# Sums of squares, the spread of the norm factors and the order of low parts in a two-layer hybrid encoder

## The chip, the cores and the metric

The kernel runs on one core of one Trainium2 chip. The metric is the device time of one execution in microseconds (us). The kernel before has a median of 2450.57 us over three runs (2447.43 to 2455.9). The engines are called PE (matmul), DVE (vector), ACT (scalar), POOL (general) and SP (issues DMAs); a DMA is called by the queue that issues it.

## The reference

The input is 256 and 512 tokens of width 1024 (one sequence each, 768 tokens together), all in fp32. There are two layers and a final norm:

```
x = x + concat_sum( sigmoid(gate_n) * branch_n( mixer_n( rmsnorm(x) ) ), n = A, B, C ) @ w_out
g, v = split( conv3( rmsnorm(x) @ w_up ) )        # each D_FF = 2816 wide
x = x + ( silu(g) * v ) @ w_down
y = rmsnorm(x) * final_g
rmsnorm(x) = x * rsqrt(mean(x*x) + 1e-6) * g
```

Mixer A is a chunked spatial gate, mixer B a windowed grouped-query attention with a sink and a relative bias, mixer C a grouped-query attention with normed and rotated queries and keys. What matters here is the norm: five times (two in each layer, one at the end, that one in two parts) the squares of x are summed over 1024 channels, a factor r is made for each token, and r is spread over all 128 partitions so that it can be multiplied onto rows of channels.

## The kernel before

Activations lie transposed: x is eight tiles of 128 channels by 768 tokens. Every fp32 product is done as three passes of a reduced format (fp32r): a value is split in a high part (`wh`, `u[:, 0]`), written by ACT as a copy, and a low part (`wl`, `u[:, 1]`), written by DVE as the difference, and PE adds high·high, high·low and low·high. For the weights a class `Stream` does this along a fixed plan: `split` (L296) issues ACT's copy (L337 or L327), `flush` (L354) issues DVE's difference (L357) and then the DMA of the next weight on SP. `dense` (L426) is the loop of matmuls L435 over k steps; it calls `flush` after one of its first k steps, and after each step lets background generators (attention, the closing norm) and delayed work (the convolution of the FFN) issue a piece. So the order in which DVE meets low parts, attention steps and convolution steps is the order in which this Python code calls them, and no scheduler changes it.

Norms. ACT squares a tile (`sumsq`, L499 and L502) and the tiles are added: in the first norm partly by DVE, partly by POOL (L504); in the others by DMAs on POOL's queue that accumulate (L508) into two sums, closed by DVE (L504, L506). `rstd_tok` (L510) sums over channels by small matmuls with ones (L514), DVE scales (L517) and POOL takes the power (L520). `rstd_bc` (L523) spreads r: for each 128 tokens DVE makes a diagonal `dg` (L534, two buffers), PE multiplies it with ones (L535, fp32), ACT copies it out (L537).

Layer phases: the token-major projections `dense_tok` (matmuls L554, evacuated by ACT L586), the attentions as background of gate and branch products, then `layer_out` (L963): evacuation L1005, and for each of four pairs of tiles operands `ua`, `ub`, `un`, `ut` (sums and differences of halves, each with a high part by ACT, L985/L987, and a low part by DVE, L988) for the FFN's up products. These are seven half-size products P1 to P7 in place of eight (matmuls L1109, evacuated by ACT L1117 and others). Up products run in 22 groups; down products (`dn`) follow in eight chunks, evacuated by DVE (L1168, in the last layer's last chunk L1158, then multiplied by the final factor in L1234). At the change of layers `prep` (L487) makes high and low parts of the new x (L488, L489) and its squares (L502).

Buffers: `page` gives one of 7 tiles of 128 x 768, `unit` one of 23 tiles twice that size, which also hold x and the operands.

Of the kernel before, what the change touches and what calls it, by code (L numbers as in the profile page):

```python
# [10 lines left out]
F32 = mybir.dt.float32  # L11
# [7 lines left out]
P = 128  # L19
# [110 lines left out]
def encoder_kernel(ctx, tc, x_d, w_d, vec_d, ln_d, rope_d, gqk_d, oneh_d, relb_d, mask_d, id_d, y_d):  # L130
# [65 lines left out]
    identr = const.tile([P, P], F32R, name="identr")  # L196
    ones = const.tile([P, P], F32, name="ones")
    neghalf = const.tile([P, 24], F32, name="neghalf")
# [4 lines left out]
    class Stream:  # L203
# [92 lines left out]
        def split(self, parts=1):  # L296
# [3 lines left out]
            if e[0] in ("pc", "down"):  # L300
# [11 lines left out]
                if e[:3] == ("down", DEPTH - 1, len(FFC) - 1):  # L312
                    k = None
                    if e[3] % 2 == 0:
                        st["keep"] = unit()
                    h, l2 = (st["keep"][:, e[3] % 2, i * HT:i * HT + w] for i in range(2))
                elif self.open is None:
                    k = j
                    hi, lo = self.pair()
                    self.open = (k, hi, lo)  # L320
                    h, l2 = hi[:, 0:w], lo[:, 0:w]
                else:
                    k, hi, lo = self.open
                    self.open = None
                    h, l2 = hi[:, 512:512 + w], lo[:, 512:512 + w]
# [100 lines left out]
    def dense(ps, hi, lo, off, ks, xs, first, last, cuts=(0, 384, 768), mid=None):  # L426
        nk = len(ks)
        for i, (kw, kx) in enumerate(ks):
# [11 lines left out]
            if mid is not None and i == 3:  # L440
                mid()
            if i == min(2, nk - 1):
                W.flush()
# [9 lines left out]
    def load_consts():  # L453
        DVE.memset(ones, 1.0)
        DVE.memset(zero, 0.0)
        DVE.memset(neghalf, -0.5)
        POOL.dma_start(out=ident, in_=id_d)
# [29 lines left out]
    def prep(x_ap, g, xu, k):  # L487
        ACT.activation(xu[:, 0], x_ap, AF.Identity, scale=g)  # L488
        DVE.scalar_tensor_tensor(xu[:, 1], x_ap, g, fl(xu[:, 0]), ALU.mult, ALU.subtract)  # L489
        if k is not None:  # L490
            sumsq(x_ap, k)

    def sumsq(x_ap, k, dve=None):

        n = x_ap.shape[-1]
        c = k % 2 if dve is None else 0
        if k == c:
            st["acc", c] = page()[:, 0:n]
            ACT.activation(st["acc", c], x_ap, AF.Square)  # L499
            return  # L500
        sq = page()[:, 0:n]
        ACT.activation(sq, x_ap, AF.Square)  # L502
        if dve is not None or k >= KD - 2:
            (POOL if dve is False else DVE).tensor_tensor(st["acc", 0], st["acc", 0], sq, ALU.add)  # L504
            if dve is None and k == KD - 2:
                DVE.tensor_tensor(st["acc", 0], st["acc", 0], st.pop(("acc", 1)), ALU.add)  # L506
# [3 lines left out]
    def rstd_tok(n=NT):  # L510
# [10 lines left out]
        st["rt"] = r  # L521

    def rstd_bc(n=NT, gap=False):  # L523
        r = st["rt"]
        bc = page(776) if gap else page()
        if gap:
            POOL.memset(bc[:, 513:514], 0.0)
        for a, b in ((0, min(n, 4)), (4, n)):
            if a >= b:
                continue  # L530
            ps = sps()
            for t in range(a, b):
                dg = sm.tile([P, P], F32, tag="dg", name=nm("dg"), bufs=2)
                DVE.tensor_scalar(dg, ident, r[:, t:t + 1], None, ALU.mult)  # L534
                PE.matmul(out=ps[:, (t - a) * P:(t - a + 1) * P], lhsT=ones, rhs=dg, start=True, stop=True)  # L535
            o = 1 + (a > 0) if gap else 0
            ACT.activation(bc[:, o + a * P:o + b * P], ps[:, 0:(b - a) * P], AF.Copy)  # L537
        st["bcg" if gap else "bc"] = bc
# [29 lines left out]
    def layer_mixers(l, xs):  # L568
# [15 lines left out]
        for c in range(2):  # L584
# [4 lines left out]
            if c == 0:  # L589
                ACT.activation(small(2)[:, 0:1], neghalf[:, 0:1], AF.Gelu_apprx_tanh)  # L590
            dense_tok(("in2", l, 512 + c * 256, 0), ("in2", l, 512 + c * 256, 1), xs, evac_v,
                      rstd_tok if c == 0 else None, kouter=c == 0)
        rt = st["rt"]
# [369 lines left out]
    def layer_out(l, mhl, x_src, x_mid):  # L963
# [29 lines left out]
        for i in range(4):  # L993
# [4 lines left out]
            for q in range(2):  # L998
# [12 lines left out]
                else:  # L1011
                    hl2(h3(xa), ub, g, slice(0, 2))
                    DVE.scalar_tensor_tensor(ta[:, HT:T], xa[:, HT:T], g, xg[:, HT:T], ALU.mult, ALU.subtract)
                    DVE.tensor_tensor(tb[:, 0:HT], ta[:, HT:T], xg[:, 0:HT], ALU.add)
                    DVE.scalar_tensor_tensor(tb[:, HT:T], xa[:, 0:HT], g, tb[:, 0:HT], ALU.mult, ALU.subtract)
                    hl2(h3(tb), un, -1.0, slice(0, 2))
                    hl2(ta[:, HT:T], ut, 1.0, i % 2)
                sumsq(xa, m)
                POOL.dma_start(out=x_mid[m], in_=xa)
# [6 lines left out]
    def layer_ffn(l, xs2, x_mid, x_spill):  # L1026
# [125 lines left out]
        def evac(c, m, cuts, ps):  # L1152
            last = c == len(FFC) - 1
            final_ = last and l == DEPTH - 1
            if final_:
                t0, t1 = cuts
                xa = st["xu"][m // 2][:, m % 2, t0:t1]
                DVE.tensor_tensor(xa, ps[:, 0, 0:t1 - t0], xa, ALU.add)  # L1158
                sumsq(xa, m)
                if t0 and m == 2:  # L1160
# [18 lines left out]
        for s in steps:  # L1179
            if s[0] == "pc":  # L1180
                piece(s[1], s[2])
                if (s[1], s[2]) == (0, "P5"):
                    rstd_tok()
                elif (s[1], s[2]) == (1, "P1"):
                    rstd_bc(gap=True)
# [33 lines left out]
    def final(xu, t0, t1):  # L1219
        n = (t1 - t0) // P  # L1220
        ph["ffn"] = "end"
        if t0 == 0:
            yield
            yield
        rstd_tok(n)
        if t0 == 0:
            yield
        yield
# [10 lines left out]
    with tc.manual_schedule():  # L1239
# [17 lines left out]
        for k in range(KD):  # L1257
# [15 lines left out]
            if k > 2:  # L1273
                sumsq(xu[(k - 3) // 2][:, (k - 3) % 2], k - 3, k % 2 == 0)
        for k in range(KD - 3, KD):
            sumsq(xu[k // 2][:, k % 2], k, True)
        del u, xu
# [137 lines left out]
```

## Time and profile before

| | us |
|---|---|
| median of three runs | 2450.57 |
| the profiled execution | 2452.3 |
| its span | 2450.1 |
| PE busy | 2393.8 |
| DVE busy | 1531.0 |
| ACT busy | 1106.6 |
| POOL busy | 268.2 |

The profile is of one execution, with a mean granted clock of 0.988. PE is busy for 98% of the span, so the time is PE's work, its idle stretches, and those stretches in which it runs on the lower of its two clocks (a granted clock of 0.5 is 1.2 GHz, of 1.0 is 2.4 GHz). A duration of a few matmuls in a row in the timeline is their span together.

### The profile page before, as it was taken

To read this page: it belongs to the slowest core of one execution; us is meant where nothing else is said; L and a number is where in the kernel's file an instruction comes from. 1 tells how busy PE (TensorE), PEld (TensorE's weight loads), DVE (VectorE), ACT (ScalarE), POOL (GpSimd) and SP (SyncE) were. 2 spreads that over 40 slices of the span, in tenths; PEclk is the share of its full clock that TensorE was granted. 3 is DMA by queue.
4 is the path that set the end of the run, shared out by engine and by line. 5 is a ranking of instruction groups with operands and counts; after the bars stand their busy time and mean duration, and the time that the engine had idled before them with its cause. 6 is when DMAs were issued, how large, how long until landed. Compare 5 with 4: busy or idle time off the path is not lost.

```text
span 2450.1 us, 38743 instructions
## 1 busy us (share of the span) xinstructions
PE 2393.8 (98%) x15030; PEld 2325.3 (95%) x15030; DVE 1531.0 (62%) x2691; ACT 1106.6 (45%) x2186; POOL 268.2 (11%) x396
## 2 busy tenths in 40 slices
PE   9999999999999999999999999999999999999996
PEld 8999999899999999999899999998999999999996
DVE  5555446554568777777645554555446688777774
ACT  4344444652355444444433543466424544444441
POOL 2000110000121111111000001100001211111101
PEclk9999999999999999999999999999999999999997
DMA  4411221112568998887722113111135699888865
GB/s 145 105 59 51 51 74 44 35 43 88 163 145 237 257 239 228 230 222 207 234 90 61 58 51 63 61 44 36 44 119 155 150 273 241 241 229 233 223 170 169
DMA packets 142439, 340.82 MB, mean 139 GB/s; under 512 B 16809, under 2 KB 34857, under 8 KB 142257
## 3 DMA queue, kind: packets, MB, share of 16 engines
q1 hardware_dynamic: 108144, 264.41, 33.0%
q0 software_dynamic: 34112, 73.95, 17.1%
q8 instruction: 118, 1.93, 0.3%
q14 instruction: 65, 0.52, 0.1%
HBM read 250.22 MB, written 58.72 MB: 126 GB/s over the span
## 4 chain that ended last, share of the span: by engine, by line
PE 85%; DMA 5%; DVE 3%; ACT 3%; issue 3%; POOL 0%; SPq 0%; POOLq 0%; DVEq 0%; ACTq 0%
PE d L435 46%; PE ga L1109 13%; PE gb L1109 9%; PE d L554 7%; PE s L799 3%; PE s L786 3%; PE s L747 3%; DMA raw<-w_pk 1%; DMA pg<-gqk 1%; PE s L659 1%; DMA qd<-qc 1%; DVE wl L357 1%; DMA qc<-w_pk 0%; DMA u<-w_pk 0%; ACT wh L327 0%
## 5 line engine op out<-in xcount | busy, mean ns | idle before, releaser
L435 PE MATMUL d<-u,wh 128*128 128x384 f32 x4512 | 996.6, 342 | 5.4 <-ACT pg L1074 5.0
L435 PEld LDWEIGHTS d<-u,wh 128*128 128x128 f32 x4512 | 788.1, 188 | 20.3 <-issue 11.0
L435 PE MATMUL d<-u,wl 128*128 128x384 f32 x2256 | 579.5, 338 | 0.0
L435 PEld LDWEIGHTS d<-u,wl 128*128 128x128 f32 x2256 | 410.7, 188 | 0.0
L1109 PE MATMUL ga<-u,wh 128*128 128x384 f32 x1408 | 364.6, 340 | 12.3 <-ACT u L1117 7.2
L357 DVE TENSOR_TENSOR wl<-raw,wh 128x512 fp32r<-128x512 f32 (+1 forms) x261 | 248.1, 951 | 200.9 <-ACT wh L337 155.4
L1109 PE MATMUL gb<-u,wh 128*128 128x384 f32 x1056 | 271.9, 339 | 0.9 <-DVE u L1119 0.9
L1109 PEld LDWEIGHTS ga<-u,wh 128*128 128x128 f32 x1408 | 257.1, 189 | 14.3 <-ACT u L1117 7.9
L554 PE MATMUL d<-wh,u 128*128 128x256 f32 x1344 | 249.1, 285 | 7.5 <-DVE pg L1168 3.2
L1109 PE MATMUL ga<-u,wl 128*128 128x384 f32 x704 | 238.9, 339 | 0.0
L554 PEld LDWEIGHTS d<-wh,u 128*128 128x128 f32 x1344 | 211.4, 191 | 9.7 <-issue 3.5
L1109 PEld LDWEIGHTS gb<-u,wh 128*128 128x128 f32 x1056 | 192.6, 189 | 1.2 <-ACT u L1083 1.2
L554 PE MATMUL d<-wl,u 128*128 128x256 f32 x672 | 190.8, 284 | 2.0 <-DVE wl L357 2.0
L337 ACT ACTIVATE wh<-raw 128x1024 fp32r<-128x1024 f32 x129 | 135.3, 1050 | 103.3 <-PE d L554 47.6
L1109 PE MATMUL gb<-u,wl 128*128 128x384 f32 x528 | 178.3, 338 | 0.0
L1168 DVE TENSOR_TENSOR pg<-d,pg 128x768 f32<-128x768 f32 x120 | 114.6, 955 | 90.8 <-PE d L435 85.6
L1046 ACT ACTIVATE pg<-u,vec 128x769 f32<-128x769 f32 x88 | 90.9, 1033 | 99.3 <-DVE u L1054 65.8
L1109 PEld LDWEIGHTS ga<-u,wl 128*128 128x128 f32 x704 | 133.3, 189 | 0.0
L554 PEld LDWEIGHTS d<-wl,u 128*128 128x128 f32 x672 | 128.6, 191 | 2.6 <-DVE wl L357 2.4
L652 DVE TENSOR_TENSOR u<-s,u 128x128 fp32r<-128x128 f32 (+1 forms) x112 | 36.8, 329 | 120.6 <-ACT u L651 120.4
L747 PE MATMUL s<-u,u 128*128 128x256 f32 (+2 forms) x384 | 99.9, 342 | 0.0
L1109 PEld LDWEIGHTS gb<-u,wl 128*128 128x128 f32 x528 | 99.7, 189 | 0.0
(197 smaller groups left out, 3142.1 us busy)
## 6 DMA issues: line engine op xcount, KB each, us to landing
raw<-w_pk SPq DMA_DIRECT2D x174, 512.0 KB, 3.7
pg<-xm SPq DMA_DIRECT2D x120, 384.0 KB, 5.1
xm<-pg SPq DMA_DIRECT2D x112, 384.0 KB, 3.9
u<-w_pk SPq DMA_DIRECT2D x96, 192.0 KB, 3.5
qa<-w_pk SPq DMA_DIRECT2D x44, 256.0 KB, 4.5
qb<-w_pk SPq DMA_DIRECT2D x44, 256.0 KB, 3.2
qc<-w_pk SPq DMA_DIRECT2D x44, 256.0 KB, 3.7
qd<-w_pk SPq DMA_DIRECT2D x44, 256.0 KB, 3.6
```

What stands on the lines that cost most here:

```text
L337: ACT.activation(hi[:, :n], t[:, :n], AF.Copy)
L357: DVE.tensor_tensor(lo, t, fl(hi), ALU.subtract)
L435: PE.matmul(out=ps[:, h, 0:b - a], lhsT=w, rhs=x[:, a:b], start=first and i == 0 and pi == 0, stop=last and i == nk - 1 and pi == 2,)
L554: PE.matmul(out=outs[t], lhsT=x, rhs=w, start=k == 0 and pi == 0 and t % 2 == 0, stop=k == KD - 1 and pi == 2, skip_group_check=True)
L652: DVE.tensor_tensor(u[:, 1, a:b], ps, fl(u[:, 0, a:b]), ALU.subtract)
L659: PE.transpose(o.bitcast(F32R) if idn is identr else o, srcs(t), idn)
L747: PE.matmul(out=ps[:, 0:w], lhsT=q, rhs=kb[:, c, lo * P:hi * P], start=c == 0, stop=c == 1)
L786: PE.transpose(ps[:, b * P:(b + 1) * P], lg[:, b * P:(b + 1) * P], ident)
L799: PE.matmul(out=ps[e * HD:(e + 1) * HD, 0:P], lhsT=vtok[:, (lo + b) * P + kv * HD:(lo + b) * P + (kv + 1) * HD], rhs=pT, start=b == 0, sto ...
L1046: ACT.activation(f, h[:, 1:770], AF.Identity, scale=cw(1, ct), bias=vec[:, VCB + ct:VCB + ct + 1])
L1109: PE.matmul(out=o, lhsT=a[:, w], rhs=x[:, b], start=p in ("P1", "P2", "P5") and kp == 0 and pi == 0, stop=kp == 3 and pi == 2, skip_group_ ...
L1168: DVE.tensor_tensor(h2(xa), ps[:, :, 0:384], h2(xa), ALU.add)
```

## The change

The eight chunks of the down product stay. Seven things change:

1. `dense` calls `flush` after the first k step where it has at most four (branch products and down chunks), not after the third or last.
2. In the first norm the squares of tiles 2 to 5 are accumulated by four DMAs on POOL's queue into two sums; DVE adds the last two and the second sum. POOL's and DVE's earlier additions go.
3. In the last layer's closing norm DVE adds all squares, and no DMA does.
4. The factors are spread by one 768-wide product on DVE, split in two fp32r parts, and four matmuls (two of 512 and two of 256 columns) with fp32r ones (`onesr`), in place of six diagonals and six fp32 matmuls. In the closing norm the matmuls stand one step of the background (three matmuls) later.
5. At the change of layers the squares lie in a `unit`, not a `page`.
6. In `layer_out` the operands of the second tile of a pair are made in another order, `un` in two halves.
7. In the last layer's last down chunk each weight has a `unit` of its own.

```diff
@@ Stream.split
                 if e[:3] == ("down", DEPTH - 1, len(FFC) - 1):
                     k = None
-                    if e[3] % 2 == 0:
-                        st["keep"] = unit()
-                    h, l2 = (st["keep"][:, e[3] % 2, i * HT:i * HT + w] for i in range(2))
+                    u = unit()
+                    h, l2 = u[:, 0, 0:w], u[:, 1, 0:w]
@@ dense
-            if i == min(2, nk - 1):
+            if i == (2 if nk > 4 else 0):
                 W.flush()
@@ load_consts
+        DVE.tensor_scalar(onesr, ones[:, 0:1].broadcast_to([P, P]), 1.0, None, ALU.mult)
@@ prep, sumsq
         if k is not None:
-            sumsq(x_ap, k)
+            sumsq(x_ap, k, new=lambda: unit(F32)[:, 0])
 
-    def sumsq(x_ap, k, dve=None):
+    def sumsq(x_ap, k, dve=False, new=None):
 
         n = x_ap.shape[-1]
-        c = k % 2 if dve is None else 0
+        c = 0 if dve else k % 2
+        sq = (new or page)()[:, 0:n]
+        ACT.activation(sq, x_ap, AF.Square)
         if k == c:
-            st["acc", c] = page()[:, 0:n]
-            ACT.activation(st["acc", c], x_ap, AF.Square)
+            st["acc", c] = sq
             return
-        sq = page()[:, 0:n]
-        ACT.activation(sq, x_ap, AF.Square)
-        if dve is not None or k >= KD - 2:
-            (POOL if dve is False else DVE).tensor_tensor(st["acc", 0], st["acc", 0], sq, ALU.add)
-            if dve is None and k == KD - 2:
+        if dve or k >= KD - 2:
+            DVE.tensor_tensor(st["acc", 0], st["acc", 0], sq, ALU.add)
+            if not dve and k == KD - 2:
                 DVE.tensor_tensor(st["acc", 0], st["acc", 0], st.pop(("acc", 1)), ALU.add)
         else:
             POOL.dma_start(out=st["acc", c], in_=sq, accum_op=ALU.add)
@@ rstd_diag, rstd_bc
+    def rstd_diag(n=NT):
+
+        r = st["rt"]
+        dh, dl = page(T, F32R)[:, 0:n * P], page(T, F32R)[:, 0:n * P]
+        dg = page()[:, 0:n * P]
+        i3 = ident.unsqueeze(1).broadcast_to([P, n, P])
+        r3 = r[:, 0:n].unsqueeze(2).broadcast_to([P, n, P])
+        DVE.tensor_tensor(dg.rearrange("p (t n) -> p t n", n=P), i3, r3, ALU.mult)
+        ACT.activation(dh, dg, AF.Copy)
+        DVE.tensor_tensor(dl, dg, fl(dh), ALU.subtract)
+        st["dg"] = dh, dl
+
     def rstd_bc(n=NT, gap=False):
-        r = st["rt"]
...
-            for t in range(a, b):
-                dg = sm.tile([P, P], F32, tag="dg", name=nm("dg"), bufs=2)
-                DVE.tensor_scalar(dg, ident, r[:, t:t + 1], None, ALU.mult)
-                PE.matmul(out=ps[:, (t - a) * P:(t - a + 1) * P], lhsT=ones, rhs=dg, start=True, stop=True)
+            for i, d in enumerate(st["dg"]):
+                PE.matmul(out=ps[:, 0:b - a], lhsT=onesr, rhs=d[:, a:b], start=i == 0, stop=i == 1)
@@ layer_mixers
-                      rstd_tok if c == 0 else None, kouter=c == 0)
+                      rstd_tok if c == 0 else rstd_diag, kouter=c == 0)
@@ layer_out, half, the branch for q == 1
-                    hl2(h3(xa), ub, g, slice(0, 2))
+                    ACT.activation(ub[:, 0:2, 0], h3(xa), AF.Identity, scale=g)
                     DVE.scalar_tensor_tensor(ta[:, HT:T], xa[:, HT:T], g, xg[:, HT:T], ALU.mult, ALU.subtract)
                     DVE.tensor_tensor(tb[:, 0:HT], ta[:, HT:T], xg[:, 0:HT], ALU.add)
+                    DVE.scalar_tensor_tensor(ub[:, 0:2, 1], h3(xa), g, fl(ub[:, 0:2, 0]), ALU.mult, ALU.subtract)
+                    hl2(tb[:, 0:HT], un, -1.0, 0)
                     DVE.scalar_tensor_tensor(tb[:, HT:T], xa[:, 0:HT], g, tb[:, 0:HT], ALU.mult, ALU.subtract)
-                    hl2(h3(tb), un, -1.0, slice(0, 2))
                     hl2(ta[:, HT:T], ut, 1.0, i % 2)
+                    hl2(tb[:, HT:T], un, -1.0, 1)
@@ layer_ffn, evac
-                sumsq(xa, m)
+                sumsq(xa, m, dve=True)
@@ layer_ffn, steps
                 if (s[1], s[2]) == (0, "P5"):
                     rstd_tok()
+                    rstd_diag()
@@ final
         rstd_tok(n)
+        rstd_diag(n)
         if t0 == 0:
+            yield
             yield
         yield
         rstd_bc(n)
@@ the kernel's start
             if k > 2:
-                sumsq(xu[(k - 3) // 2][:, (k - 3) % 2], k - 3, k % 2 == 0)
+                sumsq(xu[(k - 3) // 2][:, (k - 3) % 2], k - 3)
         for k in range(KD - 3, KD):
-            sumsq(xu[k // 2][:, k % 2], k, True)
+            sumsq(xu[k // 2][:, k % 2], k)
```

How this moves DVE's instructions is shown at three places. First the start, where the first norm's sum closes: `u` at L489 (L490 in the changed kernel) is a low part of x, `pg` at L504 and L506 are additions of squares, L517 reads the finished sum. Before:

```order
L489 SCALAR_TENSOR_TENSOR u_164<-u_99,vec_91,u_164 128x768
L357 TENSOR_TENSOR wl_168<-raw_107,wh_167 128x1024
L489 SCALAR_TENSOR_TENSOR u_176<-u_100,vec_91,u_176 128x768
L504 TENSOR_TENSOR pg_156<-pg_156,pg_179 128x768
L489 SCALAR_TENSOR_TENSOR u_182<-u_100,vec_91,u_182 128x768
L504 TENSOR_TENSOR pg_156<-pg_156,pg_188 128x768
L504 TENSOR_TENSOR pg_156<-pg_156,pg_191 128x768
L504 TENSOR_TENSOR pg_156<-pg_156,pg_194 128x768
```

In the changed kernel:

```order
L490 SCALAR_TENSOR_TENSOR u_165<-u_101,vec_92,u_165 128x768
L357 TENSOR_TENSOR wl_169<-raw_109,wh_168 128x1024
L490 SCALAR_TENSOR_TENSOR u_177<-u_102,vec_92,u_177 128x768
L490 SCALAR_TENSOR_TENSOR u_183<-u_102,vec_92,u_183 128x768
L504 TENSOR_TENSOR pg_158<-pg_158,pg_192 128x768
L506 TENSOR_TENSOR pg_158<-pg_158,pg_163 128x768
L504 TENSOR_TENSOR pg_158<-pg_158,pg_196 128x768
L357 TENSOR_TENSOR wl_228<-raw_156,wh_227 128x1024
```

The additions among the low parts are gone, and of the three that are left the first two take sums that DMAs write.

Second the windowed attention of layer 0 (time 211 to 215 before). L836 evacuates a gate product, L770 and L774 (L780 and L784 after) divide a softmax row, L756 (L766) makes the next one, L357 is the low part of a weight. Before:

```order
L836 TENSOR_TENSOR pg_2143<-d_2006,pg_733 128x768
L770 RECIPROCAL sm_2102<-sm_2102 128x1
L774 TENSOR_SCALAR pg_2100<-pg_2100,sm_2102 128x256
L756 ISA pg_2168,sm_2169<-s_2171,sd_1485,sm_576 128x256
L756 ISA sm_2169 128x1
L357 TENSOR_TENSOR wl_2147<-raw_1908,wh_2146 128x1024
```

In the changed kernel:

```order
L846 TENSOR_TENSOR pg_2137<-d_2000,pg_741 128x768
L357 TENSOR_TENSOR wl_2141<-raw_1902,wh_2140 128x1024
L780 RECIPROCAL sm_2096<-sm_2096 128x1
L784 TENSOR_SCALAR pg_2094<-pg_2094,sm_2096 128x256
L766 ISA pg_2165,sm_2166<-s_2168,sd_1479,sm_584 128x256
L766 ISA sm_2166 128x1
```

The low part has moved in front of the division, the next row's start and what follows them.

Third the end: the last rows of the first part of the closing norm. L1158 (L1170 after) adds a down product to x, L504 and L506 add squares, L517 reads the sum. Before:

```order
L1158 TENSOR_TENSOR u_22899<-d_23111,u_22899 128x512
L1158 TENSOR_TENSOR u_22900<-d_23125,u_22900 128x512
L504 TENSOR_TENSOR pg_23038<-pg_23038,pg_23136 128x512
L506 TENSOR_TENSOR pg_23038<-pg_23038,pg_23056 128x512
L1158 TENSOR_TENSOR u_22900<-d_23140,u_22900 128x512
L504 TENSOR_TENSOR pg_23038<-pg_23038,pg_23151 128x512
L517 TENSOR_SCALAR sm_23169<-ga_23164 128x4
```

In the changed kernel:

```order
L1170 TENSOR_TENSOR u_22885<-d_23102,u_22885 128x512
L504 TENSOR_TENSOR pg_23026<-pg_23026,pg_23113 128x512
L1170 TENSOR_TENSOR u_22886<-d_23116,u_22886 128x512
L504 TENSOR_TENSOR pg_23026<-pg_23026,pg_23127 128x512
L1170 TENSOR_TENSOR u_22886<-d_23130,u_22886 128x512
L504 TENSOR_TENSOR pg_23026<-pg_23026,pg_23141 128x512
L517 TENSOR_SCALAR sm_23159<-ga_23154 128x4
```

Each product is now followed by the addition of its square, and no L506 (the second sum, which DMAs filled) stands in front of the last product.

## Rows read from the trace of the kernel before

**Rows 1.** The page, part 1: busy time, share and instructions by engine.

```profile
PE 2393.8 (98%) x15030; PEld 2325.3 (95%) x15030; DVE 1531.0 (62%) x2691; ACT 1106.6 (45%) x2186; POOL 268.2 (11%) x396
```

**Rows 2.** Windows: us, busy (x instructions) by engine, granted clock, DMA share, GB/s.

```profile
20.00:25.00 5.00, 3.84 (x20) 3.84 (x21) 3.07 (x5) 4.69 (x6) 3.54 (x3) 0.66 0.14 38
...
693.00:702.00 9.00, 7.16 (x29) 7.17 (x29) 5.03 (x8) 4.41 (x10) 1.74 (x2) 0.62 0.54 139
...
1213.00:1222.00 9.00, 5.79 (x28) 5.50 (x27) 5.72 (x6) 3.92 (x5) 1.96 (x3) 0.65 0.89 244
...
2412.00:2451.00 39.00, 18.86 (x91) 17.27 (x89) 17.29 (x39) 4.92 (x11) 5.22 (x7) 0.65 0.37 104
```

**Rows 3.** Waits of PE: line, releaser, us in total, times, longest.

```profile
PE ga L514 <- DVE pg L504: 8.8, 2, 5.2
...
PE ga L1109 <- ACT u L1117: 7.2, 2, 3.6
...
PE d L435 <- ACT pg L1074: 5.0, 2, 2.5
...
PE d L554 <- DVE pg L1168: 3.2, 1, 3.2
```

**Rows 4.** Timeline, first norm, ACT, DVE, PE: start, us, instruction, [idle <-releaser].

```profile
16.71 0.83 ACT L502 ACTIVATE pg<-u 128x768 f32<-128x768 f32 x1
...
16.84 2.46 DVE L489 SCALAR_TENSOR_TENSOR u<-u,vec,u 128x768 fp32r<-128x768 f32 x1
...
22.82 3.08 DVE L504 TENSOR_TENSOR pg<-pg,pg 128x768 f32<-128x768 f32 x3 [1.72 <-POOL pg L504]
...
25.96 1.50 PE L514 MATMUL s<-ones,pg 128*128 128x2 f32 x12
...
32.76 0.38 PE L554 MATMUL d<-wh,u 128*128 128x256 f32 x1 [0.93 <-ACT u L586]
```

**Rows 5.** DMA issues: KB, median us to landing; then line L508's range.

```profile
pg<-pg POOLq DMA_DIRECT2D x12, 384.0 KB, 4.5
...
DMA to landing us min/median/max: 2.6/4.3/6.6
```

**Rows 6.** Timeline of PE: spread of factors (layer 0), last chunk's products.

```profile
63.93 0.61 PE L535 MATMUL s<-dg,ones 128*128 128x128 f32 x4
...
66.04 0.36 PE L554 MATMUL d<-wh,u 128*128 128x256 f32 x1
...
2394.45 17.99 PE L435 MATMUL d<-u,u 128*128 128x512 f32 x81
```

**Rows 7.** Timeline of DVE and PE in layer 0's windowed attention.

```profile
211.30 0.15 DVE L770 RECIPROCAL sm<-sm 128x1 f32<-128x1 f32 x1
...
213.40 1.23 DVE L357 TENSOR_TENSOR wl<-raw,wh 128x1024 fp32r<-128x1024 f32 x1 [0.40 <-ACT wh L337]
...
213.24 0.38 PE L786 MATMUL s<-ident,pg 128*128 128x128 f32 x2
```

**Rows 8.** Timeline of DVE, ACT, PE from layer 0's projection into its FFN.

```profile
691.19 0.62 DVE L1015 SCALAR_TENSOR_TENSOR pg<-u,vec,pg 128x384 f32<-128x384 f32 x1
...
691.90 1.25 ACT L985 ACTIVATE u<-pg 128x768 fp32r<-128x768 f32 x2 [2.92 <-DVE pg L1015]
...
694.84 1.01 PE L1109 MATMUL ga<-u,wh 128*128 128x384 f32 x2 [3.60 <-ACT u L1117]
```

**Rows 9.** Timeline of ACT and DVE before PE's 2.48 us wait at 1180.13.

```profile
1172.65 0.51 ACT L327 ACTIVATE wh<-u 128x384 fp32r<-128x384 f32 x1
...
1176.58 0.55 DVE L357 TENSOR_TENSOR wl<-u,wh 128x384 fp32r<-128x384 f32 x1
```

**Rows 10.** Timeline of ACT before layer 1's first matmul.

```profile
1212.51 0.84 ACT L502 ACTIVATE pg<-pg 128x768 f32<-128x768 f32 x1 [1.99 <-DMA sp<-pg]
```

**Rows 11.** Timeline of DVE in the two closing norms.

```profile
2413.29 0.69 DVE L504 TENSOR_TENSOR pg<-pg,pg 128x512 f32<-128x512 f32 x1 [3.30 <-DMA pg<-pg]
...
2437.45 0.42 DVE L506 TENSOR_TENSOR pg<-pg,pg 128x256 f32<-128x256 f32 x1 [1.34 <-DMA pg<-pg]
```

More of the change, by code (lines that the diff above doesn't have):

```diff
@@ L196, in encoder_kernel @@
     identr = const.tile([P, P], F32R, name="identr")
-    ones = const.tile([P, P], F32, name="ones")
+    ones = const.tile([P, 2], F32, name="ones")
+    onesr = const.tile([P, P], F32R, name="onesr")
     neghalf = const.tile([P, 24], F32, name="neghalf")
@@ L527, in rstd_bc @@
             POOL.memset(bc[:, 513:514], 0.0)
-        for a, b in ((0, min(n, 4)), (4, n)):
+        for a, b in ((0, min(n, 4) * P), (4 * P, n * P)):
             if a >= b:
@@ L531, in rstd_bc @@
             ps = sps()
-            for t in range(a, b):
-                dg = sm.tile([P, P], F32, tag="dg", name=nm("dg"), bufs=2)
-                DVE.tensor_scalar(dg, ident, r[:, t:t + 1], None, ALU.mult)
-                PE.matmul(out=ps[:, (t - a) * P:(t - a + 1) * P], lhsT=ones, rhs=dg, start=True, stop=True)
+            for i, d in enumerate(st["dg"]):
+                PE.matmul(out=ps[:, 0:b - a], lhsT=onesr, rhs=d[:, a:b], start=i == 0, stop=i == 1)
             o = 1 + (a > 0) if gap else 0
-            ACT.activation(bc[:, o + a * P:o + b * P], ps[:, 0:(b - a) * P], AF.Copy)
+            ACT.activation(bc[:, o + a:o + b], ps[:, 0:b - a], AF.Copy)
+        del st["dg"]
         st["bcg" if gap else "bc"] = bc
```

## The prediction

> **What bounds the kernel now.** I read the page's busy times first. PE is busy for 2393.8 of 2450.1 us; no other engine is above 62% [rows 1]. So only three things can change the time: what PE executes, where PE waits, and where it runs at the lower clock. The windows by stage show the third: granted 1.00 nearly everywhere, but 0.66 just before the first norm's sum, 0.62 at the entry to an FFN (both layers alike), 0.65 at the change of layers and 0.65 over the last 39 us [rows 2]. Each of these stands at one of PE's longer waits, listed next: 8.8 us in the two closing norms for a sum of squares, 7.2 us at the two FFN entries for ACT, 5.0 us at the end of each layer, 3.2 us at the change of layers [rows 3]. The change works on all four places and, by the order, on attention.
>
> **First norm (start): a loss, +4.8.** Before, DVE closes the sum with three additions from 22.82 on, and PE's L514 starts at 25.96; the first matmul that needs nothing from it but evacuated PSUM follows at 32.76 [rows 4]. Now two chains of two accumulating DMAs each take the additions. The square of tile 3 is ready at 16.71 + 0.83 = 17.54 [rows 4]; POOL starts its DMA some 0.3 later (an estimate). A 384 KB transfer of this kind takes 4.5 us at the median [rows 5], and the next in the chain may start only after it has landed: 17.85 + 4.5 + 0.3 + 4.5 = 27.15. Two of DVE's additions follow it at 3.08 / 3 = about 0.95 apart, so L514 starts near 29.1, 3.1 us late. What goes is POOL's addition, beside which DVE's L489 took 2.46 us [rows 4]; PE then has its inputs sooner, but ends up waiting at L514 anyway, for some 6.5 us. After a wait of 3.6 us PE ran at the lower clock for most of 9 us at 0.62 [rows 2, 3]: 3.4 us of full clock, of which I count 2.7 on work. From L514 to the end of the work that was queued before 32.76 there are 32.76 − 25.96 − 0.93 = 5.8 us of PE, so 29.1 + 5.8 + 2.7 = 37.6, against 32.76: +4.8. At the shortest landing of 2.6 L514 starts at 25.3 and, with half the clock loss, the cost is 0; at the longest of 6.6 it starts at 33.3: +9 [rows 5].
>
> The Trainium skill (SBUF — State Buffer, section "SBUF: two separate sides", the box on DVE blocking DMA) says that a DMA from POOL's queue needs its descriptors written by GpSimd, and that this stalls while DVE holds the shared port. By that rule each link could wait for one of DVE's low parts, about 1 us, and the sum would be 2 us worse. The rows give L508's landing only with DVE at work beside it, so such a stall is in the 4.5 already and I add nothing.
>
> **The spread of the factors, −2.8 −0.8.** In the mixers L535 holds PE from 63.93 to 66.04, 2.1 us, and six DVE products stand between its matmuls [rows 6]. Four fp32r matmuls over 512, 512, 256 and 256 columns cost, at 17.99 / 81 = 0.222 us for 512 [rows 6], 0.22 + 0.22 + 0.11 + 0.11 = 0.67. Their operands (a 768-wide DVE product, an ACT copy, a DVE low part, under 3 us together) can be made from 32.76 on, 31 us before the spread [rows 4, 6], so nothing waits: −1.4 in each layer. In the FFN the power is ready only shortly before the spread, and product, copy and low part then stand in front of PE in one chain; I take −0.4 in each layer, between −1 and +1.5.
>
> **Attention: low parts earlier, +2.1.** In 14 places of the branch products the order moves a low part before a softmax division. It needs ACT's high part first. At 213.40 DVE had waited for that copy already, while the division stood at 211.30: it now goes to 213.4 + 1.2, 3.3 us later, and PE's use of its row at 213.24 is only 1.9 behind the old start [rows 7]. PE is in order, so I estimate 0.8 us lost there after what the matmuls between absorb. At most places the high part is long there, the delay is the 1.2 us of one low part, and PE's next use lies 1 to 3 us behind. I take 0.15 us for each place, 2.1 together; from 0 to the full 14 × 1.23 = 17 us, the trace bounds it no closer.
>
> **Into the FFN, −3.8.** Before, the last operand's two copies start at 691.90, only after L1015 began at 691.19, and ACT's next in line (a square, a weight copy, L1117) let PE go at 694.84 [rows 8]. With L988's full low part (1 us) out of the way of the differences and `un` in halves, only the second half's copy, 1.25 / 2, stands last and starts near 691.45: PE restarts near 693.8, −1.05 in each layer. The wait of 3.6 becomes 2.5. A shorter wait may leave a shorter stretch at the low clock: of the 3.4 us that it takes there [rows 2] I count a quarter back, −0.85 in each layer, between 0 and −2.7.
>
> **End of each layer, +1.5.** PE's wait at 1180.13 (2.5) hangs on an evacuation queued on DVE behind convolution steps. The low part at 1176.58, whose high part was ready at 1172.65 + 0.51 [rows 9], now stands before those steps: about +0.65 in each layer (0.55 and its start), +0.2 together for the clock. In the other FFN groups PE's next use lies several us behind and I count zero; if that cover were gone, some 40 down products at 0.5 each would cost 20 us, which is in no range below.
>
> **Change of layers, −4.0.** At 1212.51 ACT's square had idled 1.99 us until a spill's DMA let a page go [rows 10]; behind it stood the high part of layer 1's first weight, and PE's wait of 3.2 [rows 3]. With squares in units that idle goes: −2.0. The wait that is left is 1.2. Of the 0.35 × 9 = 3.2 us that the low clock takes here [rows 2] most may come back; but before the first norm's sum a low clock stands beside short waits too [rows 2], so I count −2.0. Bounds −1 (the next page is as late) and −5.
>
> **The tail, −3.5.** DVE waited 3.30 us for an accumulating DMA at 2413.29 and 1.34 at 2437.45, with the last product's evacuation queued behind [rows 11]. With additions in place a product's chain is low part, evacuation, ACT's square and addition, each near the 0.69 of an addition [rows 11]: about 2.5 us while low parts stand between and 2.0 after, against PE's 9 × 0.222 = 2.0 [rows 6], so DVE falls behind by some 2 us at most and has nearly caught up at the last product. PE's last matmul ends at 2394.45 + 17.99 = 2412.44 [rows 6]; evacuation, square and addition of 2.0 and a backlog of 0.4 put L514 at 2414.8, a wait of 2.4 for 5.2 [rows 3]. DVE's multiplications by the factor (L1234) still hold the second part's evacuations, so not all of that returns: −1.5 at the middle, −3.5 at the end. Bounds −1.5 (DVE's backlog stays) and −5.5 (the lower clock also ends sooner).
>
> **Sum.** 4.8 − 2.8 − 0.8 + 2.1 − 3.8 + 1.5 − 4.0 − 3.5 = −6.5. Against the profiled execution (2452.3; span 2450.1) this is 2445.8; that execution lies 1.7 above the median of the runs, so the median goes to 2444.
>
> **The rivals.**
> *All clock returns.* At FFN entry and change of layers the waits fall under what costs the clock, and attention hides its low parts: −3.7 more at the entries, −1.2 at the change, −2.1, and the tail's −2: 2444 − 9 = 2435. For it: every one of these waits is shortened. Against it: 2.5 is left at the entries, as long as waits that cost clock before.
> *Gains turn into new waits.* ACT's chain at the entry ends on the square, not the copy; DVE becomes the tail's bound with three operations for each product; the freed page waits on the next spill. Terms at their small ends: 4.8 − 2.8 + 0.5 + 2.1 − 1 + 1.5 − 1 − 1.5 = +2.6, or 2453; since not all three go together, I put it midway between that and my sum: 2448.5. For it: each step has a next one close behind [rows 8, 10]. Against it: they are different engines at different places.
> *Slower: low parts hold the softmax.* One place, 14 times: DVE waits in order for ACT's high part, and PE for the row behind it. At 1.2 us in each place, the length of a low part, this costs 17 in place of 2.1: 2459. The kernel is slower than before from (6.5 + 2.1) / 14 = 0.6 us in each place, and by over 0.3% from (6.5 + 2.1 + 7.35) / 14 = 1.1. For it: DVE idles for ACT's copies at this point already [rows 7]. Against it: most high parts are ready.
> *DMA chain held by DVE* (the rule named above): L514 near 31, +2: 2446. The rows show no such stall by itself.
>
> **How the numbers follow.** A measurement of this kernel can tell 0.3%, 7.35 us, from no change: faster is below 2443.2, slower above 2457.9. My forecast has a chance of 0.46, and its own range of 2437 to 2450 lies about evenly on either side of 2443.2: 0.23 faster, 0.23 same. All clock returns: 0.19, faster. New waits: 0.18, same. DMA chain held: 0.04, same. Low parts hold the softmax: 0.13, slower. Together faster 0.42, same 0.45, slower 0.13. The range starts below the first rival and ends short of the slow one: 2433 to 2454.
>
> **What would show it.** In the changed profile: L514 at the start near 29 (my chain of DMAs right) or before 26 (wrong); L535 of 0.7 us; FFN entries near 2.5 us of wait and a granted clock there above 0.62; the first matmul of layer 1 with a wait near 1.2 at full clock; L514 in the tail with a wait under 3; in attention, waits of PE for L774's and L787's users no more than 2 us above before. I am wrong if PE's waits in attention grow by 10 us, if L514 at the start is later than 33, or if the tail's sum still waits over 4 us.

## The result and the profile after

The changed kernel is slower: 2461.2 us (median of 12 runs) against 2447.66 for the kernel before on the same chip, a ratio of 1.0055, 95% interval [1.0046, 1.0063]. That is +13.5 us where −6.5 was forecast, outside the range. The profiled execution took 2465.5 us, its span is 2463.7.

Part 1 of its page. It answers to [rows 1]: PE does 40 matmuls and 2.8 us less, and the span is 13.6 us longer, so the loss is in PE's idle time: 72.7 us of the span against 56.3.

```profile
PE 2391.0 (97%) x14990; PEld 2319.5 (94%) x14990; DVE 1535.8 (62%) x2688; ACT 1111.2 (45%) x2200; POOL 260.2 (11%) x390
```

Windows of the changed kernel, columns as in [rows 2]: the start, the entry into the FFN of layer 0, the spread of the factors behind it, the change of layers, the tail.

```profile
20.00:45.00 25.00, 13.44 (x82) 13.03 (x81) 8.02 (x13) 8.08 (x13) 5.74 (x8) 0.73 0.60 134
...
714.00:722.00 8.00, 7.17 (x45) 7.17 (x46) 4.00 (x7) 2.89 (x7) 1.73 (x2) 1.00 0.61 166
...
722.00:736.00 14.00, 10.90 (x46) 9.97 (x45) 5.44 (x9) 5.62 (x12) 4.06 (x5) 0.76 0.60 113
...
1230.00:1245.00 15.00, 12.96 (x98) 12.46 (x97) 9.98 (x11) 8.42 (x11) 2.06 (x4) 1.00 0.97 274
...
2426.00:2463.00 37.00, 20.14 (x100) 17.51 (x98) 20.38 (x43) 7.14 (x15) 1.73 (x2) 0.70 0.24 85
```

PE's longest waits, as [rows 3]:

```profile
PE s L514 <- DVE pg L504: 10.6, 1, 10.6
...
PE d L435 <- ACT pg L1086: 6.4, 2, 3.2
...
PE d L564 <- DVE wl L357: 6.2, 2, 3.9
...
PE ga L1121 <- ACT u L1129: 4.4, 2, 2.2
...
PE ga L544 <- ACT pg L531: 3.6, 2, 2.0
...
PE d L544 <- ACT pg L531: 3.6, 2, 2.9
...
PE ga L514 <- DVE pg L504: 3.5, 2, 2.0
...
PE d L564 <- DVE pg L1180: 2.0, 2, 1.2
```

The waits of [rows 3] are all shorter but one: 8.8 us for the closing sums became 3.5, 7.2 at the FFN entries 4.4, 3.2 at the change of layers is in the 2.0; 5.0 at the ends of the layers became 6.4. What is new stands beside them: 10.6 us at the first norm, 6.2 us for a low part, 3.6 us for the FFN's spread (`d L544`) and 3.6 us for the spread in the closing norm (`ga L544`; before, PE waited 1.7 us there for `dg`). And the clock moved with the waits: 0.62 at the entry is 1.00, but behind the spread, where it was full speed, it is 0.76; at the change of layers 0.65 is 1.00.

PE runs the same matmuls in the same order in both kernels, but for the spread. So the n-th matmul of one can be set against the n-th of the other, from PE's timelines, and the lag shows where time goes. It sets one execution against one; each lies some 4.5 us above its kernel's median. "Evacuation" is the copy that empties PE's output buffer (PSUM).

| place (first matmul there) | before | after | lag |
|---|---|---|---|
| first matmul that waits for an evacuation behind the first norm | 32.76 | 43.67 | +10.9 |
| behind the spread, layer 0 | 66.04 | 75.56 | +9.5 |
| gate products, before any moved low part | 88.00 | 98.36 | +10.4 |
| windowed attention | 180.61 | 194.25 | +13.6 |
| behind the tables' DMA | 315.36 | 333.87 | +18.5 |
| second attention | 489.98 | 511.62 | +21.6 |
| behind the FFN entry, layer 0 | 700.12 | 717.75 | +17.6 |
| behind the FFN's spread | 711.96 | 733.94 | +22.0 |
| end of the layer | 1181.44 | 1202.14 | +20.7 |
| layer 1, products | 1223.71 | 1239.48 | +15.8 |
| behind the spread, layer 1 | 1271.16 | 1286.20 | +15.0 |
| second attention | 1693.96 | 1713.00 | +19.0 |
| at the FFN entry, layer 1 | 1899.64 | 1917.46 | +17.8 |
| first closing sum | 2417.63 | 2431.58 | +14.0 |
| end of the span | 2450.1 | 2463.7 | +13.6 |

Four steps up make the result: the start, the attentions, the place behind the tables' DMA (transfers `pg<-gqk` on POOL's queue, which both kernels issue alike for mixer C; more at the end of the experiments) and the FFN's spread in layer 0. Within layer 1's FFN the lag also falls to +13.4 at 2039.87 and rises to +16.8 at 2081.84, behind a wait of 1.82 us for a weight's copy that no other run's list of waits has. The start first: POOL, then DVE and PE (start, us, instruction, idle before and releaser).

```profile
16.23 0.87 POOL L508 DMA_DIRECT2D pg<-pg  x1 [14.20 <-ACT pg L499]
...
17.78 0.85 POOL L508 DMA_DIRECT2D pg<-pg  x1 [0.68 <-ACT pg L499]
...
24.43 0.84 POOL L508 DMA_DIRECT2D pg<-pg  x1 [5.81 <-DMA pg<-pg]
...
26.28 0.84 POOL L508 DMA_DIRECT2D pg<-pg  x1 [1.00 <-DMA pg<-pg]
```

```profile
28.40 0.96 DVE L504 TENSOR_TENSOR pg<-pg,pg 128x768 f32<-128x768 f32 x1 [9.04 <-DMA pg<-pg]
...
31.18 0.96 DVE L506 TENSOR_TENSOR pg<-pg,pg 128x768 f32<-128x768 f32 x1 [1.82 <-DMA pg<-pg]
...
33.26 2.72 PE L514 MATMUL s<-ones,pg 128*128 128x2 f32 x12 [10.63 <-DVE pg L504]
...
43.67 0.39 PE L564 MATMUL d<-wh,u 128*128 128x256 f32 x1 [0.93 <-ACT u L596]
```

The first accumulating DMA was issued at 16.23, and the next of its chain could go only at 24.43; the second, from 17.78, held its follower to 26.28. So each took close to 8 us, not 4.5 [rows 5]; the chain of waits (start, us, what) has the second and the fourth:

```profile
17.78 7.97 DMA pg<-pg
...
26.28 4.81 DMA pg<-pg
```

DVE idled 9.04 us for the chain, L514 started at 33.26 instead of 25.96 [rows 4], after a wait of 10.63, and PE worked off what followed at the lower clock: 10.4 us from L514 to the matmul that waits for an evacuation, 6.8 before. This is the one of the prediction's three signs of being wrong that came: L514 later than 33.

A place in the windowed attention, DVE and PE:

```profile
186.88 1.23 DVE L357 TENSOR_TENSOR wl<-raw,wh 128x1024 fp32r<-128x1024 f32 x1 [1.95 <-ACT wh L337]
...
188.02 0.15 DVE L780 RECIPROCAL sm<-sm 128x1 f32<-128x1 f32 x1
...
189.02 0.44 PE L796 MATMUL s<-ident,pg 128*128 128x128 f32 x2 [1.42 <-DVE sm L766]
...
190.15 0.50 PE L757 MATMUL s<-u,u 128*128 128x256 f32 x2 [0.69 <-ACT pg L797]
```

The low part waited 1.95 us for ACT's high part, and the division behind it came at 188.02; PE waited 1.42 us for its row and 0.69 for the next copy, and the clock fell behind that, as the window of 191 to 195 shows (before, PE was busy without a gap over these matmuls, at 1.00):

```profile
191.00:195.00 4.00, 4.00 (x20) 3.22 (x20) 2.51 (x9) 1.64 (x6) 0.00 (x0) 0.57 0.04 14
```

The attention's waits of PE in the list of waits:

```profile
PE s L796 <- DVE sm L771: 2.4, 3, 1.0
...
PE s L796 <- DVE pg L784: 2.2, 3, 1.0
...
PE s L757 <- ACT pg L797: 1.6, 3, 0.7
...
PE s L796 <- DVE sm L766: 1.4, 1, 1.4
```

With low parts as before only the second of these four lines stands in that list (2.2 us, below); the other three are 5.4 us that the new order made, short of the 10 that the prediction named as a sign; smaller waits and the lower clock at the first place make up the rest of what attention lost.

The spread in the FFN of layer 0: POOL, DVE, ACT, PE.

```profile
723.62 0.84 POOL L275 DMA_DIRECT2D qd<-qc  x1 [3.27 <-DMA qc<-w_pk]
...
724.18 1.66 POOL L520 TENSOR_TENSOR sm<-sm,neghalf 128x6 f32<-128x6 f32 x1
...
725.88 0.96 DVE L530 TENSOR_TENSOR pg<-ident,sm 128x768 f32<-128x768 f32 x1 [5.11 <-POOL sm L520]
...
726.87 0.84 ACT L531 ACTIVATE pg<-pg 128x768 fp32r<-128x768 f32 x1 [8.55 <-DVE pg L530]
...
727.76 0.80 PE L544 MATMUL d<-pg,onesr 128*128 128x512 f32 x1 [2.90 <-ACT pg L531]
```

POOL waits for a weight transfer before it takes the power at 724.18. This was so before, at 704.23: POOL is only 1.7 us nearer, by the lag (+19.95 for +21.6), while PE comes 4.0 us nearer. Product, copy and low part follow the power one after the other, and PE, which now comes at full clock from the entry, waits 2.90 us and then loses clock.

The change of layers and the tail gain what was forecast. PE's first matmul of layer 1 waits 1.17 us at full clock:

```profile
1235.06 0.36 PE L564 MATMUL d<-wh,u 128*128 128x256 f32 x1 [1.17 <-DVE pg L1180]
```

In the tail DVE's additions wait only for ACT's squares, and PE's waits for the sums are 2.0 and 1.6 where they were 5.2 and 3.6. Of these 5.3 us PE gives back 1.9 in the waits for the spread (3.6 for 1.7) and 1.5 in one wait for an evacuation (L1170; 3.2 for 1.7).

```profile
2430.84 0.69 DVE L504 TENSOR_TENSOR pg<-pg,pg 128x512 f32<-128x512 f32 x1 [0.74 <-ACT pg L499]
...
2444.89 0.42 DVE L1170 TENSOR_TENSOR u<-d,u 128x256 f32<-128x256 f32 x1
...
2431.58 1.05 PE L514 MATMUL ga<-ones,pg 128*128 128x2 f32 x8 [1.96 <-DVE pg L504]
...
2452.93 0.58 PE L514 MATMUL ga<-ones,pg 128*128 128x2 f32 x4 [1.58 <-DVE pg L504]
```

### The profile page after: what moved, and what is told of

The parts are those of the page before. It is cut to its first block, busy times and chain, and to the rows that moved or that the text cites. A ratio compares the mean times of both kernels' runs of the same rounds, so it can differ in the third digit from the quotient of the medians.

```text
span 2463.7 us, 38666 instructions
## 1 busy us (share of the span) xinstructions
PE 2391.0 (97%) x14990; PEld 2319.5 (94%) x14990; DVE 1535.8 (62%) x2688; ACT 1111.2 (45%) x2200; POOL 260.2 (11%) x390
## 4 chain that ended last, share of the span: by engine, by line
PE 85%; DMA 5%; DVE 4%; ACT 3%; issue 3%; POOL 0%; POOLq 0%; SPq 0%; DVEq 0%; ACTq 0%
PE d L435 46%; PE ga L1121 13%; PE gb L1121 10%; PE d L564 7%; PE s L809 3%; PE s L796 2%; PE s L757 2%; DMA raw<-w_pk 1%; DVE wl L357 1%; DMA qc<-w_pk 1%; DMA pg<-gqk 1%; PE s L669 1%; DMA pg<-pg 1%; ACT wh L337 0%; DMA qd<-qc 0%
## 5 line engine op out<-in xcount | busy, mean ns | idle before, releaser
L357 DVE TENSOR_TENSOR wl<-raw,wh 128x512 fp32r<-128x512 f32 (+1 forms) x261 | 248.2, 952 | 224.0 <-ACT wh L337 180.9
L768 ACT ACTIVATE pg<-pg,sm 128x257 f32<-128x257 f32 (+1 forms) x96 | 52.5, 547 | 109.2 <-DVE sm L766 105.0
```

The costliest lines, as they stand in the source:

```text
L357: DVE.tensor_tensor(lo, t, fl(hi), ALU.subtract)
L768: ACT.activation(lg, lg, AF.Exp, bias=mn, scale=-1.0, accum_out=su)
```

## The experiments

All ratios are to the kernel before on the same chip, with 95% intervals; the changed kernel stands at 1.0055, and one thousandth is 2.45 us.

### What each of two edits costs

Sums of the first norm as before:

```diff
-        if dve or k >= KD - 2:
+        if old is not None:
+            (POOL if old is False else DVE).tensor_tensor(st["acc", 0], st["acc", 0], sq, ALU.add)
+        elif dve or k >= KD - 2:
```

> The changed kernel with the first norm's sums made as before (POOL and DVE additions, no accumulating DMA). Theory: the start alone lost 10.6 us (PE stood 10.6 us later after the first norm than before), because two accumulating DMAs at once share the same DMA engines and each needs about 8 us; so this run is about 10.5 us below the changed kernel: 2450.5, L514 near 26. Rival: the changed kernel's profiled execution had a late DMA by chance and the start costs the forecast 4.8: 2456.4.

Measured: 1.0025 [1.0013, 1.0037], 7.4 us below the changed kernel, between the two. L514 starts at 25.81 and the matmul behind the next evacuation at 32.61, so the start gives back all of its 10.9; some 3 us are lost again from 88 on, where PE now waits for an evacuation and the clock falls.

Low parts as before:

```diff
-            if i == (2 if nk > 4 else 0):
+            if i == min(2, nk - 1):
```

> The changed kernel with low parts issued after the third or last k step as before. Theory: low parts in front of the softmax cost 6.4 us in layer 0 and 4.0 in layer 1, and 1.3 at the ends of the layers: 2449.5. Rival: what was lost in attention hangs on the tables' DMA (low part waiting 3.9 us at 331) and on chance, not on this order: no more than 2 us, 2459.

Measured: 0.9997 [0.9986, 1.0008], 14.2 us below the changed kernel. The theory holds, and the loss is rather more than 11.7. The rival falls: this kernel waits even longer behind the tables' DMA and is faster all the same. PE's waits for a low part and in the attention:

```profile
PE d L564 <- DVE wl L357: 7.4, 2, 4.0
...
PE s L796 <- DVE pg L784: 2.2, 3, 1.0
```

Both of these edits together:

> Both undone at once. Theory: the two losses add up, so about 22 us below the changed kernel, 2439, and 8 to 9 us below the kernel before (the gains at the change of layers, the tail, the entry into the FFN and the spread). Rival, that these gains are given back later when the losses are gone: between 2444 and 2448.

Measured: 0.9964 [0.9950, 0.9978], 8.8 us below the kernel before and 22 below the changed one: the losses add, and what is left of the change gains what was forecast for those parts.

Low parts early in the down products alone:

```diff
-            if i == (2 if nk > 4 else 0):
+            if i == (2 if nk >= 4 else 0):
```

> The changed kernel with the earlier low part kept for the branch products' neighbours with at most three k steps only (the down products), and the branch products as before. Theory: the loss lies in attention, so this is within 2 us of the run with all low parts as before: 2450.5. Rival: the loss is in the FFN's down products: about as the changed kernel, 2460.

Measured: 1.0005 [0.9994, 1.0016], 12.3 us below the changed kernel. So the loss lies in the branch products, beside the attentions; the down products' part is about 2 us by the medians, with intervals that touch, and PE's wait at the ends of the layers stays at 6.4 us here, where it is 5.0 with all low parts as before.

### Why the accumulating DMAs came late

One chain only, tiles 3 and 5 by DVE:

```diff
+        elif half and c == 1:
+            DVE.tensor_tensor(st["acc", 1], st["acc", 1], sq, ALU.add)
         else:
             POOL.dma_start(out=st["acc", c], in_=sq, accum_op=ALU.add)
```

> The changed kernel, but in the first norm only the squares of tiles 2 and 4 are accumulated by DMA (one chain, never two transfers at once) and those of 3 and 5 by DVE. Theory: two accumulating DMAs at once share the same engines; alone each lands in 4.0 to 4.8 us instead of 8, so the chain ends near 25.5 and L514 starts near 27.5 to 28 instead of 33: about 6 us below the changed kernel (1.003 of before). Rival: weight loads or the start itself slow such a DMA, each still needs 7 to 8: L514 near 33 or later and no gain.

Measured: 1.0050 [1.0036, 1.0065], and L514 at 32.00. My theory fell. POOL's timeline:

```profile
16.40 0.87 POOL L510 DMA_DIRECT2D pg<-pg  x1 [14.37 <-ACT pg L499]
...
24.56 0.85 POOL L510 DMA_DIRECT2D pg<-pg  x1 [7.29 <-DMA pg<-pg]
```

With no second transfer beside it the first still let the next go only at 24.56, after 7.3 us of waiting. Something else slowed it. In the changed kernel DVE's low part of a weight ends at 16.44 and lets a buffer go, and SP at once issues the load of the next 512 KB of weights. The DMA queues from 16 to 19.5 us (packets, MB, share of 16 engines) show what moves then:

```profile
16.47 0.33 SPq L246 DMA_DIRECT2D raw<-w_pk  x1
```

```profile
q1 hardware_dynamic: 53, 0.22, 51.7%
q8 instruction: 1, 0.02, 2.3%
```

No packet of POOL's queue (q0, as the next run shows) moves in these 3.5 us, though the first accumulating DMA was issued at 16.23.

Two runs take the load apart from a first use. The low part, and with it the load, after the low parts of x:

```diff
             if k == 5:
                 W.split()
-                W.flush()
...
         for k in range(KD - 3, KD):
             sumsq(xu[k // 2][:, k % 2], k)
+            if k == KD - 3:
+                W.flush()
```

> The changed kernel, with the one low part of a weight at the start (and the 512 KB weight load issued behind it) put after the low parts of x, so that this load no longer runs beside the first two accumulating DMAs. Theory: the first two took 7.7 and 8.0 us because that load shares the DMA engines from 17.5 to 20; without it they land in about 5 us and L514 starts 3 to 5 us sooner, near 29. Rival: an accumulating DMA at the start takes 7.7 by itself (its first use, or DVE's work beside it): L514 stays at 32 to 33.

```profile
16.41 0.87 POOL L508 DMA_DIRECT2D pg<-pg  x1 [14.38 <-ACT pg L499]
...
17.96 0.85 POOL L508 DMA_DIRECT2D pg<-pg  x1 [0.67 <-ACT pg L499]
...
20.89 0.84 POOL L508 DMA_DIRECT2D pg<-pg  x1 [2.09 <-ACT pg L499]
...
23.27 0.84 POOL L508 DMA_DIRECT2D pg<-pg  x1 [1.53 <-ACT sm L600]
```

Now the third DMA goes at 20.89 and the fourth at 23.27, so the first two landed within 4.5 and 5.3 us instead of close to 8, and from 16 to 19.5 POOL's queue moves:

```profile
q0 software_dynamic: 111, 0.34, 52.9%
```

They had stood behind the weight load. DVE ran the same two low parts of x beside them in both kernels (from 16.78 and 18.34 there, from 16.96 and 18.52 here), so the rival that DVE holds the chain does not explain the 8 us. Why the load kept POOL's queue back, and did not only share with it, no run shows. The load, now issued at 20.75, falls beside the last two, which hold DVE until 27.06 and 28.95: 6.2 and 5.7 us from issue to DVE's start, though DVE is idle for most of it, for 4.0 and 4.9 in the changed kernel. The last one in the chain of waits:

```profile
23.27 5.59 DMA pg<-pg
```

L514 starts at 31.02, 2.2 us sooner and not the 3 to 5 expected, and PE waits 2.7 us at 20.73 for the low part that is now late. The time is the changed kernel's, 1.0049 [1.0027, 1.0071].

A tiny accumulating DMA ahead:

```diff
+        wa = small(8)
+        wb = small(8)
...
+        POOL.dma_start(out=wa, in_=wb, accum_op=ALU.add)
         for k in range(KD):
```

> The changed kernel with a tiny accumulating DMA (128 x 8, to a tile nobody reads) issued on POOL some 8 us ahead of the first. Theory of a first use: the four real ones then land in about 4.5 us each and L514 starts near 29. Theory of sharing the engines with the weight load: no difference, L514 at 32 to 33.

```profile
32.20 2.72 PE L514 MATMUL s<-ones,pg 128*128 128x2 f32 x12 [9.56 <-DVE pg L504]
```

L514 at 32.20, a ratio of 1.0056 [1.0040, 1.0072]: within 1.1 us of the changed kernel, so a first use explains at most that.

### What is worth keeping

No DMA and no POOL in the first norm, low parts as before:

```diff
-                sumsq(xu[(k - 3) // 2][:, (k - 3) % 2], k - 3)
+                sumsq(xu[(k - 3) // 2][:, (k - 3) % 2], k - 3, dve=True)
```

> Low parts as before, and all squares of the first norm added by DVE (no POOL addition, no DMA). Theory: POOL's two additions of 2.4 us each, beside which a DVE low part took 2.46 instead of 1.0, cost at least as much as the two additions of 0.95 that DVE gets more; L514 near 25, the kernel 1 us below the run with both undone: 0.9959 of before. Rival: DVE is the bound of the start (busy all of 8 to 16 us) and L514 comes 2 us later than 26: 0.9972.

Measured: 0.9957 [0.9944, 0.9970]. L514 starts at 24.51, 1.45 us sooner than before, as the theory says; in the time the step from 0.9964 is inside the intervals.

```profile
24.51 1.50 PE L514 MATMUL s<-ones,pg 128*128 128x2 f32 x12 [0.83 <-DVE pg L504]
```

The spread in the FFN later:

```diff
-                elif (s[1], s[2]) == (1, "P1"):
+                elif (s[1], s[2]) == (0, "P4"):
                     rstd_bc(gap=True)
```

> Start sums and low parts as before, and in the FFN the factors' spread one product (2.1 us of PE) later. Theory: in the FFN PE now comes to the spread before the power on POOL and the three-step chain behind it are done; it waits 1 to 2.9 us and then runs at half clock for some 2 to 2.5 us of loss. With the spread later the wait goes and with it that stretch: 2 to 4 us below the run with both undone, 0.995. Rival: the wait only moves on, to DVE's scaling or to the next copy: within 1 us of it.

Measured: 0.9972 [0.9960, 0.9983], no gain on 0.9964 (2 us more by the medians, inside the intervals). The rival names what happens: the wait at the spread goes, and PE waits 1.92 us at 712.00 for ACT's next copies (L1139), four such waits being 6.0 us in all.

These two edits together, with low parts as before:

> All squares of the first norm added by DVE, low parts as before, spread in the FFN later. If the theories of the two runs before hold, their gains add: 0.9947 of before or less. Rival: the sum of the parts is not reached, 0.996.

Measured: 0.9954 [0.9942, 0.9966], the fastest of all by a hair, and not to be told from the run without the later spread; the rival's 0.996 and the theory's 0.9947 both lie inside the interval.

Three edits on the kernel before (units for squares, additions by DVE in the closing norm, operands' order), without the new spread:

```diff
-            sumsq(x_ap, k)
+            sumsq(x_ap, k, new=lambda: unit(F32)[:, 0])
...
-                sumsq(xa, m)
+                sumsq(xa, m, True)
```

> The kernel before with three of the seven edits alone: squares in units at the change of layers, DVE's additions in the last layer's closing norm, and the operands' order in the output projection; first norm, low parts and spread as before. Theory: these are the edits that gain, 3.9 us at the change of layers, 3.2 in the tail, 1.9 at each FFN entry (in layer 0 given back at the spread): 0.9961 of before. Rival: the tail and the entry need the new spread too: 0.998.

Measured: 0.9960 [0.9945, 0.9976], the theory's number. These three together carry the gain; no run takes them apart, so what each brings is read from the lags alone.

The same, with the first norm's sums on DVE:

```diff
-                sumsq(xu[(k - 3) // 2][:, (k - 3) % 2], k - 3, k % 2 == 0)
+                sumsq(xu[(k - 3) // 2][:, (k - 3) % 2], k - 3, True)
```

> The same, and all squares of the first norm added by DVE. Theory: another 1.5 us (the run with that sum on DVE was 0.9957 against 0.9964 with the old sums): 0.9955. Rival: without the new spread in the mixers (1.3 us in each layer) it stays behind the best run so far, 0.9965.

Measured: 0.9965 [0.9949, 0.9980]. It does not tell the two apart: the interval takes in both, and in this execution the tables' DMA alone cost 3.9 us of wait.

That DMA makes the one large step in the lag table that no edit names. Behind it a low part waits in DVE's queue, at 331.00 in the changed kernel; PE's wait for low parts there and in layer 1 came to 6.2 us in the changed kernel, 2.0 before, 7.4 with low parts as before (above), and in the run with all squares on DVE:

```profile
PE d L564 <- DVE wl L357: 2.7, 2, 1.7
```

These numbers follow no edit. Whether they are chance or come from where other transfers fall is open: each kernel has one trace.

## Why the prediction was wrong

*The sum had the right terms and two wrong sizes (the landing of a DMA at the start, the cost of a low part in attention), and one step, the FFN's spread, failed outright.* Term by term, from the lags:

- **First norm, +4.8: it was +10.9.** I took 4.5 us for each DMA from [rows 5], the median of transfers elsewhere in the program, and gave 6.6 as the longest. The stretch of the start was not looked at for what else moves there: a 512 KB weight load that the end of DVE's own low part sets off at 16.47. The chain of two was right: 8.0 and 4.8 us in the later chain put L514 at 33.26. That this is my upper end's 33.3 is luck, since I had 6.6 for both. Behind L514 I was 1.9 short: the lower clock cost 3.6 us, not 2.7, and I set the end of the queued work without the wait of 0.93 against 32.76, which has it. (An addition's 3.08 / 3 is 1.03, not 0.95, too: 0.2 us.) The run with the load moved away shows that the load is the cause, and the one with a small DMA ahead leaves at most 1.1 us for a first use. The rival that DVE holds the chain named a wrong cause; it gave L514 near 31.
- **Spread in the mixers, −2.8: it was −1.05 and −1.75, right in sum** (lags of +10.6 at 40.47 to +9.5, and of +16.8 at 1241.82 to +15.0).
- **Attention, +2.1: about +9.5**, 6.4 in layer 0 and 3.1 in layer 1, with the steps behind the tables' DMA (4.9 at 331.00 and 0.9 at 1534.08) left out; 12.3 us by the run that undoes it there alone. I put 0.15 us on each of 14 places; the mean was 0.68. The rival that a low part holds the softmax named place and mechanism, and its bound of 0.6 us for a slower kernel was passed. I gave it 0.13. What was wrong was to average slack over places: most lose nothing, five lose 1.2 to 3.3 us each, since DVE stands in order behind ACT's high part, and a wait of 1.4 at 189 brings a stretch at the lower clock with it.
- **Into the FFN −3.8 and spread −0.8: these were one term, not two.** The entries gained 4.0 in layer 0 and 1.9 in layer 1, in sum more than forecast. But the step "product, copy and low part then stand in front of PE in one chain; I take −0.4 in each layer" failed in layer 0, beyond its upper end of +1.5: PE came 4.0 us sooner to a power that POOL, held by a weight transfer, takes 1.7 us sooner, waited 2.90 us, and the clock that had been saved at the entry was lost behind the spread: +4.4. I had the chain's 2.9 us of product, copy and low part and did not move PE's arrival with the gain that I had just booked.
- **End of each layer, +1.5:** PE's wait grew from 2.5 to 3.2 us in both, as worked out.
- **Change of layers, −4.0: −3.9; tail, −3.5: −3.2** (lags of +20.7 to +16.8 at 1241.82, and from +16.8 at 2081.84 to the end). Right in size, and the run with three edits, at 0.9960, agrees with the sum. Inside the tail the parts were not: the middle gained 2.9 where I had 1.5, and the rest only 0.3 where I had 2.0, since the waits for the spread and for an evacuation grew by 3.4.

So −6.5 became +13.6 between the profiled executions, 20 us more: about 6 from the start, 7 from attention, 5 from the FFN's spread and 6 behind the DMA of the tables, less 2 at the FFN entries and some 3 within the FFNs. How much of the step behind the tables the medians hold, and how much of it belongs to attention's 12.3, stays open.

## What to carry to other kernels

Look at what sets off a transfer: an instruction on another engine that frees a buffer can put a weight load beside the DMA that you just put on the critical path, and the median of the same transfer elsewhere is no price for it. Where an engine runs in order, price a moved instruction at each place by the releaser of that place, not by an average slack; a few places pay it all. And when PE is made to come sooner, move its arrival through the next waits before booking the gain.

## What the runs showed of the hardware

Two accumulating DMAs of 384 KB, 1.5 us apart, landed within 4.5 and 5.3 us when the weight load was moved away. Issued 0.2 us ahead of that load of 512 KB, one took 7 to 8 us, alone or with a second one, and POOL's queue moved no packet until 19.5; two issued while the load was on its way took about 6. A DMA of the same 192 KB tables took 11.8 to 19.5 us from issue to landing in the changed kernel, 11.8 to 17.4 before, with nothing changed about it. The clock fell after waits of PE of 1.4 and 0.7 us close together (at 189), while one of 1.17 at 1235.06 and one of 0.88 at 1241.82, 6.8 us apart, left it at 1.00; before, the window of the first, with a wait of 3.2, had 0.65.
